# Two encoder layers on one core: layer 0's keys pass DRAM once as float32 and are split on chip

## The chip, the core and the metric

The kernel runs on one core of a Trainium2 chip. Time is the device time of one execution in microseconds (us). The engines have names in the profile: PE is TensorE (matmuls; PEld its weight loads), DVE is VectorE, ACT is ScalarE, POOL is GpSimd, SP is SyncE, whose queue issues nearly all transfers, in order. Tiles lie in SBUF as 128 partitions (rows) by some columns.

## The reference

Two layers of a streaming encoder, for 1024 prompt positions and for 8 streams of 16 new positions with cached keys and values. All is float32.

```python
# layer 0: two attentions side by side, 8 heads of 64 each
qa, ka, va, qb, kb, vb, fa = split(rmsnorm(x) @ w_in_even)
# a: causal, with a forget gate; c = cumsum(log_sigmoid(fa + b_forget))
s = qa @ ka.T / 8 + (c_q - c_k);  s = where(kpos <= qpos, s, -inf)
# b: a band of 8 chunks of 64 to the left, with a bias by clipped distance
s = qb @ kb.T / 8 + bias;         s = where(in_band, s, -inf)
o = softmax(s) @ v;  x += concat(oa, ob) @ w_out;  x += swiglu(rmsnorm(x))
# layer 1: 16 query heads in 2 groups, one key and value head a group, window 128
s = q @ k.T / 8 + t5_bias;  softmax with a learned sink;  x += ... (as above)
y = rmsnorm(x)        # the new keys, values and gates are returned too
```

## The kernel before

Float32 accuracy comes from products in a faster 32-bit format (F32R): an operand is split into a high part (a cast) and a low part (the difference), and three products are summed. `passes` issues them (L191 to L193) for projections and feed-forward. The order of instructions on each engine is fixed when the kernel is built: the program lists steps with costs, `merge` interleaves lists by them, and a scheduler then places the instructions.

Layer 0 starts with the projections. `proj_k` (L369) handles one pair of heads of keys, 128 rows by 1024 positions: it copies the result out, stores it as an output, splits it, and stores the high and the low part to DRAM (`kh`, `kl`). `attn_load` (L456) later loads one head: q (64 rows high, 64 rows low); the keys' high part twice, one below the other; the low part; for kind a also q's high part again (`bt`) and four gate rows each for `bt` and `kl` from `cpd`; for kind b the bias instead. Most tiles have two buffers. Values of two heads share a tile (`vp`) and are split by GpSimd (L484, L485).

`score_step` (L490) takes 128 query rows against up to 512 keys with two products into one sum: L505, q high and low against the doubled high keys (128 rows), and L507, q high against the low keys. For kind a that second product has 68 rows (64 and the gate rows); for kind b it has 64. Then come the softmax (L442 on VectorE, L445 on ScalarE), transposes (L544), a split of the weights (L548, L549), and the products with the values (L574, L575); GpSimd applies the reciprocal sums (L593), which pass DRAM (`rds`). `sample_steps` (L656) is merged between: cached keys and values of one stream (`skt`, `svt`, 1 MB each), bias of kind a (`sbi`, L679), scores (L695), and the values product L720, whose last block has the 16 new positions (`svn`) and 16 rows.

Layer 1's attention is `c_steps` (L834). Keys and values of a group of 8 query heads are loaded when it starts; these tiles have one buffer. Its list has 194 entries, about three to each of 64 units (one pair of query heads by 128 positions). The first `cut` entries, 24/32 of them (L1591), are merged with six of the eight q projections, the rest runs behind. Here the score products are L777 and L778, the transposes L794, and the values products L809 and L810.

Of the kernel before, what the change touches and what calls it, by code (L numbers as in the profile page):

```python
# [11 lines left out]
F32 = mybir.dt.float32  # L12
# [7 lines left out]
P = 128  # L20
# [9 lines left out]
HD = 64  # L30
# [8 lines left out]
VB = 1  # L39
APART = 1  # L40
# [20 lines left out]
def model(ctx: ExitStack, tc: tile.TileContext, I, O):  # L61
# [62 lines left out]
    kh = {k: dr.tile([512, NP], F32, name=f"kh_{k}") for k in "ab"}  # L124
    kl = {k: dr.tile([512, NP], F32, name=f"kl_{k}") for k in "ab"}
    kh["c"] = dr.tile([P, NP], F32, name="kh_c")
    kl["c"] = dr.tile([P, NP], F32, name="kl_c")
# [20 lines left out]
    def nm(s):  # L148
        uid[0] += 1
        return f"{s}_{uid[0]}"  # L150
# [218 lines left out]
    def proj_k(src, act, pool, out, dst_hi, dst_lo, dst_sample, get=ps_any):  # L369
        def finish(o, c0, c1):  # L370
            w = min(c1, NP) - c0
            kf = pool.tile([P, c1 - c0], F32, name=nm("kf"), tag="kf", bufs=2)
            A.copy(kf, o[:, :c1 - c0])
            S.dma_start(out[:, c0:c1], kf)
            kh_ = pool.tile([P, c1 - c0], F32R, name=nm("khs"), tag="sth", bufs=2)
            kl_ = pool.tile([P, c1 - c0], F32R, name=nm("kls"), tag="stl", bufs=2)
            A.copy(kh_[:, :w], o[:, :w])
            V.tensor_tensor(kl_[:, :w], o[:, :w], kh_[:, :w], ALU.subtract)
            S.dma_start(dst_hi[:, c0:c0 + w], f32(kh_)[:, :w])
            S.dma_start(dst_lo[:, c0:c0 + w], f32(kl_)[:, :w])  # L380
            if c1 > NP:
                S.dma_start(dst_sample, kf[:, w:w + NS])

        return chunk_steps(src, act, get, finish, 1)
# [71 lines left out]
    def attn_load(pool, kind, h):  # L456


        tl = lambda z: pool.tile([P, NP], F32R, name=nm(z), tag=z, bufs=2)
        q, kh_, kl_, v = (tl(z) for z in ("q", "kh", "kl", "v"))  # L460
        v = v.rearrange("p (a b) -> p a b", b=P)
        if h % 2 == 0:
            marks["vp"] = pool.tile([P, 8, P], F32, name=nm("vp"), tag="vp", bufs=VB)
        vp = marks["vp"]
        n = 4 if kind == "a" else 0
        rows = slice(h * HD, (h + 1) * HD)
# [4 lines left out]
        bt = pool.tile([P, NP], F32R if n else F32, name=nm("bt"), tag="bt", bufs=2)  # L471
        if n:
            S.dma_start(f32(bt)[n:n + HD], qs[kind][h][:HD])
            S.dma_start(f32(bt)[:n], cpd[h, 0])
            S.dma_start(f32(kl_)[:n], cpd[h, 1])
            q2, kl2, bias = bt[:n + HD], kl_[:n + HD], None
        else:
            S.dma_start(bt[:, :640], I["bias_b"][h])
            G.tensor_scalar(bt[:, :640], bt[:, :640], -1.0, 1.0, ALU.mult, ALU.mult)
# [3 lines left out]
        vp = vp[:, :, h % 2 * HD:(h % 2 + 1) * HD]  # L483
# [172 lines left out]
    def sample_steps(pool, qbd, nbs):  # L656
        st = {}

        def head(kind, hd):
            for z, src in (("q", qsm), ("k", ksm)):  # L660
                hd[z] = pool.tile([P, 4, NS], F32, name=nm(z + "all"), tag=z + "all")
                S.dma_start(hd[z], src[kind])
# [22 lines left out]
        def load_v(kind, b, un):  # L685
            un["vn"] = vn = pool.tile([16, 512], F32, name=nm("svn"), tag="svn", bufs=2)
            S.dma_start(un["vt"], I[f"cache_{kind}_v"][b])
            S.dma_start(vn, vsm[kind][b * 16:(b + 1) * 16, :])
# [13 lines left out]
        def trans(un):  # L702
            un["p"] = pts = pool.tile([P, 5, P], F32, name=nm("spt"), tag="spt", bufs=1)
# [8 lines left out]
        def values(un):  # L712

            op, pts = un["o"], un["p"]
            for kb in range(5):
                for p in range(4):
                    c = slice(p * 32, (p + 1) * 32)
                    lhs = pts[:, kb, c] if kb < 4 else pts[:16, 4, c]
                    rhs = un["vt"][:, kb, p * P:(p + 1) * P] if kb < 4 else un["vn"][:, p * P:(p + 1) * P]
                    E.matmul(op[c, :P], lhs, rhs, start=kb == 0, stop=kb == 4, skip_group_check=True)  # L720
# [113 lines left out]
    def c_steps(pool, qt):  # L834
# [3 lines left out]
        def load(j):  # L838
            kv = j // 4
            if j % 4 == 0:  # L840
                kh_ = pool.tile([P, NP], F32R, name=nm("kh"), tag="kh", bufs=1)
                kl_ = pool.tile([P, NP], F32R, name=nm("kl"), tag="kl", bufs=1)
                v = pool.tile([P, 8, P], F32R, name=nm("v"), tag="v", bufs=1)
# [629 lines left out]
    def unit(ki, p, pool, w=None):  # L1473

        kind = "ab"[ki]
        if p < 4:
# [4 lines left out]
                      kh[kind][p * P:(p + 1) * P], kl[kind][p * P:(p + 1) * P], ksm[kind][:, p, :])  # L1481
# [289 lines left out]
```

## Time and profile before

| | |
|---|---|
| Median of 3 runs | 2781.97 us (2778.57 to 2789.56) |
| Profiled execution, own time | 2780.07 us |
| its span in the profile | 2778.3 us |
| TensorE busy, weight loads busy | 2639.6 us (95%), 2525.9 us (91%) |
| VectorE, GpSimd, ScalarE busy | 60%, 44%, 41% |
| Mean granted TensorE clock | 0.969 of full |
| DMA | 357.65 MB, 129 GB/s over the span |

How to read it: a matmul's end is modelled, so successive starts say more of its cost than its length, and a gap may hide inside "busy". The granted clock is the share of 2.4 GHz that TensorE was given. In a view by stage a row has from:to in us, the length, then busy us and (x instructions) of PE, PEld, DVE, ACT and POOL, the clock, the share of 16 DMA engines, and GB/s. A row in order of time has start, length, engine, line, operation, output<-inputs, shape and, in brackets, the idle time before it and what ended that. A row of waits has total us, times and the longest. A row of groups has count, then busy us, mean ns and idle before.

### The profile page before, as it was taken

What the parts mean: (1) busy time and instruction counts of PE and PEld (TensorE: products, weight loads), DVE (VectorE), ACT (ScalarE), POOL (GpSimd) and SP (SyncE); (2) the same over time, 40 slices, a digit from 0 to 9 for tenths busy, and PEclk for the clock granted to TensorE, in tenths of its full rate; (3) what the DMA queues carried; (4) which work ended last, traced back from release to release, by engine and by line L of the source; (5) the groups of instructions that cost most, each with busy time, mean ns of one, the idle gap of its engine ahead of it and who ended that gap; (6) DMA issues with size and microseconds to landing.
All of it is one profiled execution on the core that took longest, in us unless ns stands there. A gap on an engine that the chain in (4) does not pass through costs nothing.

```text
span 2778.3 us, 52629 instructions
## 1 busy us (share of the span) xinstructions
PE 2639.6 (95%) x19774; PEld 2525.9 (91%) x19774; DVE 1661.7 (60%) x3583; ACT 1139.7 (41%) x2510; POOL 1229.6 (44%) x1120
## 2 busy tenths in 40 slices
PE   8999998998989999999999998869799999999997
PEld 7999976777989999999999998869799999999997
DVE  7110275766685565655667767854956555566666
ACT  5221376776342222223333466754432222233333
POOL 4212122232543343434997532233444344448984
PEclk9999998999989999999999999989999999999998
DMA  5546587885222332326443132332123222355432
GB/s 161 171 136 205 175 232 235 261 278 173 66 74 86 96 104 81 102 83 233 148 119 104 60 113 86 103 104 74 71 71 102 85 98 96 94 179 200 119 96 77
DMA packets 209840, 357.65 MB, mean 129 GB/s; under 512 B 27816, under 2 KB 134448, under 8 KB 207536
## 3 DMA queue, kind: packets, MB, share of 16 engines
q1 hardware_dynamic: 204976, 349.55, 40.6%
q10 hardware_dynamic: 4608, 4.72, 0.5%
q8 instruction: 156, 2.56, 0.4%
q14 instruction: 100, 0.82, 0.1%
HBM read 252.22 MB, written 101.95 MB: 127 GB/s over the span
## 4 chain that ended last, share of the span: by engine, by line
PE 77%; DVE 9%; DMA 7%; issue 2%; ACT 2%; POOL 1%; SPq 1%; DVEq 0%; ACTq 0%; POOLq 0%
PE ps L191 21%; PE ps L192 21%; PE ps L193 20%; PE ps L544 2%; PE ps L507 2%; DVE hf L281 1%; PE ps L505 1%; PE ps L397 1%; PE ps L396 1%; PE ps L398 1%; DMA oraw<-od 1%; PE ps L574 1%; DVE pg L285 1%; PE ps L575 1%; DVE h L281 1%
## 5 line engine op out<-in xcount | busy, mean ns | idle before, releaser
L191 PE MATMUL ps<-pg,wh 128*128 128x288 f32 x3200 | 955.9, 300 | 22.5 <-ACT wh L284 9.9
L192 PE MATMUL ps<-pg,wh 128*128 128x288 f32 x3200 | 951.9, 298 | 3.0 <-POOL pg L285 2.0
L193 PE MATMUL ps<-pg,wh 128*128 128x288 f32 x3200 | 937.1, 296 | 1.4 <-DVE wh L285 1.3
L191 PEld LDWEIGHTS ps<-pg,wh 128*128 128x128 f32 x3200 | 606.3, 190 | 28.3 <-ACT wh L284 11.6
L192 PEld LDWEIGHTS ps<-pg,wh 128*128 128x128 f32 x3200 | 608.2, 190 | 5.4 <-POOL pg L285 2.8
L193 PEld LDWEIGHTS ps<-pg,wh 128*128 128x128 f32 x3200 | 604.0, 190 | 2.7 <-DVE wh L285 2.1
L285 POOL TENSOR_TENSOR wh<-wr,wh 128x1024 fp32r<-128x1024 f32 (+1 forms) x96 | 232.8, 2429 | 327.7 <-ACT wh L284 327.4
L284 ACT CAST wh<-wr 128x1024 fp32r<-128x1024 f32 (+2 forms) x156 | 160.9, 1036 | 249.7 <-PE ps L193 219.7
L191 PE MATMUL ps<-hh,wh 128*128 128x288 f32 x832 | 246.1, 301 | 4.2 <-ACT hh L284 3.1
L192 PE MATMUL ps<-hl,wh 128*128 128x288 f32 x832 | 247.4, 299 | 2.5 <-DVE hl L285 2.3
L193 PE MATMUL ps<-hh,wh 128*128 128x288 f32 x832 | 244.9, 296 | 0.0
L285 POOL TENSOR_TENSOR pg<-pg,pg 128x576 fp32r<-128x576 f32 x126 | 197.1, 1579 | 47.4 <-ACT pg L284 47.1
L1335 DVE TENSOR_TENSOR x<-x,ps 128x288 f32<-128x288 f32 x384 | 158.1, 447 | 89.3 <-PE ps L193 74.8
L284 ACT CAST pg<-pg 128x576 fp32r<-128x576 f32 (+1 forms) x134 | 90.4, 702 | 246.1 <-PE ps L193 106.4
L285 POOL TENSOR_TENSOR wh<-x,wh 128x1024 fp32r<-128x1024 f32 x42 | 100.9, 2403 | 151.4 <-ACT wh L284 151.4
L191 PEld LDWEIGHTS ps<-hh,wh 128*128 128x128 f32 x832 | 156.5, 190 | 8.4 <-ACT hh L284 5.0
L192 PEld LDWEIGHTS ps<-hl,wh 128*128 128x128 f32 x832 | 158.0, 190 | 4.6 <-DVE hl L285 3.6
L193 PEld LDWEIGHTS ps<-hh,wh 128*128 128x128 f32 x832 | 157.9, 190 | 0.1
L285 POOL TENSOR_TENSOR x<-wr,x 128x512 fp32r<-128x512 f32 x44 | 58.7, 1334 | 210.7 <-ACT x L284 210.7
L1191 DVE TENSOR_TENSOR u<-p,ps 128x288 f32<-128x288 f32 x176 | 78.9, 448 | 112.6 <-PE ps L193 112.4
L549 DVE TENSOR_TENSOR pl<-ps,ph 128x512 fp32r<-128x512 f32 (+1 forms) x152 | 92.3, 611 | 33.8 <-ACT ph L548 33.1
L191 PE MATMUL ps<-x,wh 128*128 128x288 f32 x352 | 105.5, 300 | 5.5 <-DVE x L1195 5.3
(298 smaller groups left out, 6166.1 us busy)
## 6 DMA issues: line engine op xcount, KB each, us to landing
wr<-w_ffn_in SPq DMA_DIRECT2D x88, 512.0 KB
hds<-hd SPq DMA_DIRECT2D x252, 144.0 KB
pg<-hds SPq DMA_DIRECT2D x126, 288.0 KB
wd<-w_ffn_out SPq DMA_DIRECT2D x36, 512.0 KB
wr<-w_out SPq DMA_DIRECT2D x22, 512.0 KB
xd<-x SPq DMA_DIRECT2D x16, 576.0 KB
x<-xd SPq DMA_DIRECT2D x16, 576.0 KB
svt<-cache_a_v SPq DMA_DIRECT2D x8, 1024.0 KB
```

Source lines behind the costliest of these rows:

```text
L191: E.matmul(out, wh_, xh_, start=first and i == 0, stop=False, skip_group_check=seen)
L192: E.matmul(out, wh_, xl_, start=False, stop=False, skip_group_check=seen)
L193: E.matmul(out, wl_, xh_, start=False, stop=last and i == n - 1, skip_group_check=seen)
L281: V.scalar_tensor_tensor(out, src, gains[:, gi, k:k + 1], rs, ALU.mult, ALU.mult)
L284: A.copy(hi, src)
L285: eng.tensor_tensor(lo, src, hi, ALU.subtract)
L396: E.matmul(o[:, :width], xh_[:, k], wts[k][0], start=k == 0, stop=False)
L507: E.matmul(sp[:, :w], q2[:, qt], kl2[:, k0:k0 + w], start=False, stop=not dg)
L544: E.transpose(pt[:, col:col + P], tl[:, (kb - kb0) * P:(kb - kb0 + 1) * P], ident)
L549: V.tensor_tensor(fl, pt[:, lo_:hi_], fh, ALU.subtract)
L1191: V.tensor_tensor(st[n, q], st["p1", q], st["x", q][:, :QW], ALU.add)
L1335: V.tensor_tensor(z, z, o, ALU.add)
```

## The change

Layer 0's keys are stored once, as float32 (`ks`), from the tile that also goes to the output. A pair of heads is loaded as one tile (`kp`, two buffers), and GpSimd makes the doubled high part and the low part of each head from it. For kind a the copy of q comes from q's tile, and the gate rows move to rows 64 to 67. For kind b rows 64 to 127 of the low part are set to zero, and the second product runs over all 128 rows. The sample tiles for the 16 new positions get 128 rows, zeroed once at the start. In layer 1 the tiles of keys and values get a second buffer, and `cut` becomes 27/32. The scratch for dynamic DMA is set to 1024.

```diff
@@ proj_k
             S.dma_start(out[:, c0:c1], kf)
+            if c1 > NP:
+                S.dma_start(dst_sample, kf[:, w:w + NS])
+            if dst_lo is None:
+                S.dma_start(dst_hi[:, c0:c0 + w], kf[:, :w])
+                return
             kh_ = pool.tile([P, c1 - c0], F32R, name=nm("khs"), tag="sth", bufs=2)
...
@@ attn_load
         if h % 2 == 0:
+            marks["kp"] = kp = pool.tile([P, NP], F32, name=nm("kp"), tag="kp", bufs=KB)
+            S.dma_start(kp, ks[kind][h * HD:(h + 2) * HD])
             marks["vp"] = pool.tile([P, 8, P], F32, name=nm("vp"), tag="vp", bufs=VB)
...
-        for r in range(2):
-            S.dma_start(f32(kh_)[r * HD:(r + 1) * HD], kh[kind][rows])
-        S.dma_start(f32(kl_)[n:n + HD], kl[kind][rows])
...
-            S.dma_start(f32(bt)[n:n + HD], qs[kind][h][:HD])
-            S.dma_start(f32(bt)[:n], cpd[h, 0])
-            S.dma_start(f32(kl_)[:n], cpd[h, 1])
-            q2, kl2, bias = bt[:n + HD], kl_[:n + HD], None
...
+            S.dma_start(f32(bt)[HD:HD + 4], cpd[h, 0])
+            S.dma_start(f32(kl_)[HD:HD + 4], cpd[h, 1])
...
-            q2, kl2, bias = q[:HD], kl_[:HD], bt
...
+        for r in range(2):
+            G.tensor_copy(kh_[r * HD:(r + 1) * HD], kp[half])
+        G.tensor_tensor(kl_[:HD], kp[half], kh_[half], ALU.subtract)
+        if kind == "a":
+            G.tensor_copy(bt[:HD], q[:HD])
+            q2, kl2, bias = bt[:HD + 4], kl_[:HD + 4], None
+        else:
+            G.memset(f32(kl_)[HD:], 0.0)
+            G.tensor_scalar(bt[:, :640], bt[:, :640], -1.0, 1.0, ALU.mult, ALU.mult)
+            q2, kl2, bias = q, kl_, bt
...
@@ sample_steps
+        vnew = [pool.tile([P, 512], F32, name=f"svn{i}") for i in range(2)]
+        pts = pool.tile([P, 5, P], F32, name="spt")
+        for z in vnew + [pts[:, 4]]:
+            G.memset(z, 0.0)
...
-                    lhs = pts[:, kb, c] if kb < 4 else pts[:16, 4, c]
...
@@ c_steps
-                kh_ = pool.tile([P, NP], F32R, name=nm("kh"), tag="kh", bufs=1)
+                kh_ = pool.tile([P, NP], F32R, name=nm("kh"), tag="kh", bufs=2)
...
@@ model
-        cut = len(cst) * 24 // 32
+        cut = len(cst) * 27 // 32
```

The scheduler gives every engine a new order in these stages. Three places follow; numbers behind a name tell buffers of one tile apart.

The first place is SyncE's queue in kind a, where the fifth head is loaded. Before:

```order
L482 DMA vp_4931<-vs_a 128x8x128
L467 DMA q_4927<-qs_a 128x1024
L594 DMA od_123<-ob_4681 64x512
L469 DMA kh_4928<-kh_a 64x1024 x2
L470 DMA kl_4929<-kl_a 64x1024
L473 DMA bt_4936<-qs_a 64x1024
L474 DMA bt_4936<-cpd 4x1024
L475 DMA kl_4929<-cpd 4x1024
L669 DMA skt_5065<-cache_a_kt 128x4x512
```

And with the change:

```order
L471 DMA q_4770<-qs_a 128x1024
L535 DMA rdb_4561<-rds_a 64x512
L474 DMA bt_4778<-cpd 4x1024
L475 DMA kl_4772<-cpd 4x1024
L681 DMA skt_4908<-cache_a_kt 128x4x512
L121 DMA rds_a<-rt_4511 4x32 x4
L699 DMA svt_4909<-cache_a_v 128x2048
L467 DMA kp_5452<-ks_a 128x1024
```

The head's keys are no longer in this piece: its pair was loaded earlier, and the `kp` here is that of the seventh and eighth head. The two gate loads have no other load of their tiles ahead of them.

The second place is SyncE's queue in layer 1's attention, around the second group's keys (`kh`, `kl`) and values (`v`). Before, they stand among the loads and stores of later units:

```order
L172 DMA wr_22744<-w_out 128x1024
L830 DMA od_124<-ou_20714 128x512
L845 DMA kh_21133<-kh_c 64x1024
L846 DMA kl_21134<-kl_c 64x1024
L845 DMA kh_21133<-kh_c 64x1024
L846 DMA kl_21134<-kl_c 64x1024
L850 DMA bt_21555<-bias_c 128x2x256
```

With the change, right behind the first group's:

```order
L857 DMA v_19392<-vs_c 128x8x128
L860 DMA bt_19398<-bias_c 128x2x256
L860 DMA bt_19717<-bias_c 128x2x256
L855 DMA kh_20918<-kh_c 64x1024
L856 DMA kl_20919<-kl_c 64x1024
L855 DMA kh_20918<-kh_c 64x1024
L856 DMA kl_20919<-kl_c 64x1024
L364 DMA qsm_c<-qf_19387 128x128
L857 DMA v_20920<-vs_c 128x8x128
L171 DMA wr_21692<-w_qc 128x1024
```

They moved ahead of the weights of a q projection (`w_qc`) and of all of the first group's stores.

The third place is GpSimd's queue in kind a. Before, a head's work there is only its values:

```order
L670 COPY skt_5065<-kall_4207 128x4x16
L672 COPY qbd_3931<-qall_4205 64x4x16 x2
L593 TENSOR_TENSOR ob_4819<-ou_4685,rdb_4717 64x2x128 x2
L679 TENSOR_TENSOR sbi_5071<-sbi_5071,cqs 128x528
L484 CAST v_4930<-vp_4931 128x8x64
L680 TENSOR_TENSOR sbi_5071<-sbi_5071,mask_79 128x16
L485 TENSOR_TENSOR v_4930<-vp_4931,v_4930 128x8x64
```

With the change:

```order
L484 COPY bt_4443<-q_4438 64x1024
L691 TENSOR_TENSOR sbi_4316<-sbi_4316,cqs 128x528
L691 TENSOR_TENSOR sbi_4615<-sbi_4615,cqs 128x528
L482 TENSOR_TENSOR kl_4440<-kp_4092,kh_4439 64x1024
L491 CAST v_4441<-vp_4094 128x8x64
L600 TENSOR_TENSOR ob_4525<-ou_4337,rdb_4350 64x2x128 x2
L481 CAST kh_4771<-kp_4774 64x1024 x2
L682 COPY skt_4908<-kall_4053 128x4x16
```

The fourth head's low keys (`kl_4440`) stand behind two steps on the sample bias (`sbi`), and the fifth head's high keys (`kh_4771`) behind a step that needs reciprocals from DRAM (`rdb`).

## Rows read from the trace of the kernel before

**Rows 1.** The page, part 1: busy us, share of span, instructions of each engine.
```profile
PE 2639.6 (95%) x19774; PEld 2525.9 (91%) x19774; DVE 1661.7 (60%) x3583; ACT 1139.7 (41%) x2510; POOL 1229.6 (44%) x1120
```

**Rows 2.** Busy time by stage, columns as told with the profile above.
```profile
200.00:340.00 140.00, 140.00 (x1109) 139.01 (x1108) 16.16 (x47) 34.39 (x84) 23.75 (x16) 1.00 0.61 185
340.00:500.00 160.00, 144.17 (x1216) 112.14 (x1216) 108.40 (x339) 109.33 (x265) 45.86 (x85) 0.91 0.82 236
500.00:660.00 160.00, 159.92 (x1296) 114.40 (x1295) 112.75 (x383) 117.21 (x302) 48.38 (x77) 1.00 0.79 240
660.00:710.00 50.00, 38.59 (x258) 36.69 (x257) 23.59 (x33) 26.34 (x45) 23.37 (x19) 0.86 0.63 193
...
1710.00:1730.00 20.00, 14.32 (x97) 13.54 (x96) 10.12 (x37) 9.63 (x30) 3.69 (x13) 0.83 0.48 128
...
1790.00:1860.00 70.00, 43.20 (x244) 38.02 (x244) 45.10 (x136) 41.02 (x113) 18.05 (x48) 0.76 0.42 127
...
380.00:390.00 10.00, 10.00 (x86) 8.02 (x85) 9.28 (x33) 9.30 (x23) 1.07 (x1) 1.00 0.89 286
```

**Rows 3.** TensorE's waits, 340 to 660 us: total us, times, longest.
```profile
PE ps L507 <- DMA kl<-cpd: 8.7, 3, 4.3
```

**Rows 4.** The chain of waits, 420 to 432 us: start, us, what.
```profile
421.42 8.05 DMA kl<-kl_a
...
429.48 1.85 DMA kl<-cpd
```

**Rows 5.** TensorE's matmuls in order of time, in kind a and kind b.
```profile
348.14 0.34 PE L505 MATMUL ps<-kh,q 128*128 128x384 f32 x1
348.31 0.34 PE L507 MATMUL ps<-kl,bt 68*128 68x384 f32 x1
348.49 0.60 PE L544 MATMUL ps<-ident,t 128*128 128x128 f32 x4
...
571.00 0.34 PE L505 MATMUL ps<-kh,q 128*128 128x384 f32 x1
...
571.63 0.38 PE L505 MATMUL ps<-kh,q 128*128 128x256 f32 x1
...
576.11 0.42 PE L505 MATMUL ps<-kh,q 128*128 128x384 f32 x1
576.46 0.44 PE L507 MATMUL ps<-kl,q 64*128 64x384 f32 x1
576.83 0.55 PE L544 MATMUL ps<-ident,t 128*128 128x128 f32 x3
```

**Rows 6.** Weight loads: the group of L507, 500 to 660 us; one of svn.
```profile
L507 PEld LDWEIGHTS ps<-kl,q 64*128 64x128 f32 x96 | 17.5, 183 | 15.3 <-issue 9.5
...
570.42 0.15 PEld L720 LDWEIGHTS ps<-svn,spt 16*32 16x32 f32 x8 [0.20 <-issue]
```

**Rows 7.** GpSimd's groups by shape, 200 to 660 us.
```profile
L285 POOL TENSOR_TENSOR wh<-wr,wh 128x1024 fp32r<-128x1024 f32 x9 | 21.6, 2409 | 71.5 <-ACT wh L284 71.5
L485 POOL TENSOR_TENSOR v<-vp,v 128x512 fp32r<-128x512 f32 x16 | 20.5, 1282 | 0.4
L484 POOL CAST v<-vp 128x512 fp32r<-128x512 f32 x16 | 9.7, 612 | 23.2 <-DMA vp<-vs_a 17.5 <-DMA vp<-vs_b 2.3 <-PE ps L507 1.8
...
L670 POOL COPY skt<-kall 128x64 f32<-128x64 f32 x16 | 3.7, 235 | 1.4 <-PE ps L695 1.4
```

**Rows 8.** Layer 1 on TensorE: two matmuls, and busy time in projections (hh) alone.
```profile
1724.03 1.01 PE L777 MATMUL ps<-kh,q 128*128 128x128 f32 x3 [5.65 <-DMA kh<-kh_c]
...
1824.72 0.28 PE L810 MATMUL ps<-pl,v 128*128 128x256 f32 x1
...
1625.00:1790.00 165.00, 82.68 (x387) 0.98 0.26 82
```

**Rows 9.** GpSimd's waits, 340 to 660 us: total us, times, longest.
```profile
POOL sbi L679 <- DMA sbi<-csd: 45.1, 6, 13.2
POOL ob L593 <- DMA rdb<-rds_a: 43.0, 8, 11.2
```

More of the change, by code (lines that the diff above doesn't have):

```diff
@@ L39 @@
 VB = 1
+KB = 2
 APART = 1
@@ L123, in model @@
     qs = {k: dr.tile([8, P, NP], F32, name=f"qs_{k}") for k in "ab"}
[L124 to L127, printed above, removed]
+    ks = {k: dr.tile([512, NP], F32, name=f"ks_{k}") for k in "ab"}
+    kh, kl = ({"c": dr.tile([P, NP], F32, name=f"{z}_c")} for z in ("kh", "kl"))
     vs = {k: dr.tile([P, 8, 4, P], F32, name=f"vs_{k}") for k in "ab"}
@@ L462, in attn_load @@
         if h % 2 == 0:
+            marks["kp"] = kp = pool.tile([P, NP], F32, name=nm("kp"), tag="kp", bufs=KB)
+            S.dma_start(kp, ks[kind][h * HD:(h + 2) * HD])
             marks["vp"] = pool.tile([P, 8, P], F32, name=nm("vp"), tag="vp", bufs=VB)
[L464 to L466 removed]
+        kp, vp = marks["kp"], marks["vp"]
+        half = slice(h % 2 * HD, (h % 2 + 1) * HD)
         S.dma_start(f32(q), qs[kind][h])
[L468 to L476 removed]
+        bt = pool.tile([P, NP], F32R if kind == "a" else F32, name=nm("bt"), tag="bt", bufs=2)
+        if kind == "a":
+            S.dma_start(f32(bt)[HD:HD + 4], cpd[h, 0])
+            S.dma_start(f32(kl_)[HD:HD + 4], cpd[h, 1])
         else:
             S.dma_start(bt[:, :640], I["bias_b"][h])
[L479 to L480 removed]
         if h % 2 == 0:
             marks["q"] = S.dma_start(vp, vs[kind][:, :, h // 2, :])
[L483 removed]
+        for r in range(2):
+            G.tensor_copy(kh_[r * HD:(r + 1) * HD], kp[half])
+        G.tensor_tensor(kl_[:HD], kp[half], kh_[half], ALU.subtract)
+        if kind == "a":
+            G.tensor_copy(bt[:HD], q[:HD])
[4 more added lines that the diff above has]
+            q2, kl2, bias = q, kl_, bt
+        vp = vp[:, :, half]
         G.tensor_copy(v[:, :, :HD], vp)
@@ L685, in load_v @@
         def load_v(kind, b, un):
-            un["vn"] = vn = pool.tile([16, 512], F32, name=nm("svn"), tag="svn", bufs=2)
+            un["vn"] = vn = vnew[b % 2]
             S.dma_start(un["vt"], I[f"cache_{kind}_v"][b])
-            S.dma_start(vn, vsm[kind][b * 16:(b + 1) * 16, :])
+            S.dma_start(vn[:16], vsm[kind][b * 16:(b + 1) * 16, :])
         def scores(kind, b, c, un):
@@ L712, in values @@
         def values(un):
-            op, pts = un["o"], un["p"]
+            op = un["o"]
             for kb in range(5):
@@ L717, in values @@
                     c = slice(p * 32, (p + 1) * 32)
-                    lhs = pts[:, kb, c] if kb < 4 else pts[:16, 4, c]
                     rhs = un["vt"][:, kb, p * P:(p + 1) * P] if kb < 4 else un["vn"][:, p * P:(p + 1) * P]
-                    E.matmul(op[c, :P], lhs, rhs, start=kb == 0, stop=kb == 4, skip_group_check=True)
+                    E.matmul(op[c, :P], pts[:, kb, c], rhs, start=kb == 0, stop=kb == 4, skip_group_check=True)
             un["of"] = of = pool.tile([P, P], F32, name=nm("sof"), tag="sof", bufs=1)
@@ L1480, in unit @@
         return proj_k(I["w_k"][ki * 4 + p], act, pool, O[f"{kind}_kt"][p * P:(p + 1) * P],
-                      kh[kind][p * P:(p + 1) * P], kl[kind][p * P:(p + 1) * P], ksm[kind][:, p, :])
+                      ks[kind][p * P:(p + 1) * P], None, ksm[kind][:, p, :])
     flat = lambda ls: [s_ for l in ls for s_ in l]
```

9 lines of the change are left out of this document (3 added, 6 removed).

## The prediction

> **What bounds the kernel now.** I read four views in this order: the page, busy time by stage, TensorE's waits, and single instructions in time order. The page gives TensorE 95% of the span and no other engine more than 60% [rows 1]. So only TensorE's lost time counts: waits, slow clock, and gaps inside what the profile still calls busy. By stage [rows 2] the feed-forward part that fills most of the span is not touched, and three stages are. In the first half of layer 0's attention (340 to 500 us, the heads of kind a, whose matmuls have 68 rows) TensorE is busy 144.2 of 160 us at a mean granted clock of 0.91. In the second half (500 to 660, kind b) it is busy 159.9 of 160 at 1.00, so nothing but TensorE seems to bind there. In layer 1's attention it is 14.3 of 20 at 0.83 in one piece (1710 to 1730), and 43.2 of 70 at 0.76 where that attention ends (1790 to 1860).
>
> In the first of these, TensorE's largest waits have one cause: three waits, 8.7 us, for the four gate rows that are loaded into the tile of the keys' low parts [rows 3]. The chain of waits shows why. The 256 KB load of the low parts takes 8.05 us, the load of gate rows into the same tile starts only when it has landed (1.85 us more), then the matmul runs [rows 4]. SyncE issues in order, so whatever stands behind that load waits too.
>
> **64-row matmuls.** In kind b each score product is a 128-row matmul (L505) and then a 64-row one (L507). For a pair of 384 columns the starts are 576.11, 576.46 and, of the matmul after, 576.83: 0.72 us; from 571.00 to 571.63 it is 0.63. The same pair in kind a, with 68 rows, goes 348.14, 348.31, 348.49: 0.35 us [rows 5]. All three stretches run at full granted clock. So the 64 rows cost 0.28 to 0.37 us a pair, mean 0.32, inside time that counts as busy; the weight loads of L507 show part of it as idle of "issue" (9.5 us over the stage) [rows 6]. There are 96 of them in kind b, all in this stage: 96 x 0.32 = 31 us. The change makes them 128 rows, with zeros below. The sample products with 16 rows (svn) show the same gap of 0.20 us going in [rows 6]; 16 units x 0.20 = 3 us. Together 34 us of TensorE.
>
> Two statements of the Trainium skill bear on this and disagree. "TensorE: Matmul & The Clock Gate", section "Why this matters for your kernels", has it that a matmul with few rows takes as long as one with 128; by that, this part is worth 0 and the sum below would be 20 us instead of 45. "TensorEngine Tiling (Array Packing)", section "Tiling Modes", says that a change of tiling mode drains the engine; by that, the 34 us go. The rows side with the second.
>
> Will the other engines follow? ScalarE is busy 117.2 of those 160 us and VectorE 112.8 [rows 2]; in 126 us ScalarE would be at 93%. The row of 380 to 390 has both at 93% with TensorE at 10.0 of 10 [rows 2], so it can be done for a while, but over eight heads some waits must come up. I take 25, with 34 and 13 as ends: at 13 the stage would take 147 us, with ScalarE at 80%.
>
> **Keys once, split on chip.** Removed loads: for a head of kind a 2 x 256 KB high parts, 256 KB low parts and 256 KB of q (64 rows of 1024 floats each) become half of a 512 KB tile that serves two heads, 768 KB less; for kind b 512 KB less. 8 x 1280 KB = 10.2 MB, at the 236 to 240 GB/s of these stages [rows 2] some 43 us of transfers that ran beside the work. The gate rows now go into tiles that no other load writes, and the SyncE queue has no load before them to wait for (first place shown from the order). So the three waits of 8.7 us should go. The granted clock of this half costs up to 144.2 x 0.09 = 13 us on top of 15.8 us idle, 28 in all. I take the 8.7, a third of the clock's 13, and give 3 back for the new work on GpSimd: 10 us. Ends: 28 if every stall goes, and -10 if GpSimd's queue makes up for all of it.
>
> The new work on GpSimd for a head is two casts, a subtraction and a copy (kind b: a zero fill) of 1024 elements each. The rows of 512 elements are 612 ns for the cast and 1282 for the subtraction, of 64 elements 235 ns for a copy, of 1024 elements 2409 ns for a subtraction [rows 7]. So a cast or copy of 1024 is near 0.61 + 512 x (0.612 - 0.235)/448 = 1.04 us, a head 3 x 1.04 + 2.41 = 5.5 us, sixteen heads 88. A zero fill of this size has no row; it reads nothing, so I bound it by 0 and the copy's 1.04, and take 1.04. GpSimd is busy 45.9 and 48.4 of 160 us in the two halves [rows 2]; with 44 more in each it is at 56 to 73%. That it is in time is the assumption that carries most risk (below).
>
> In the projections 32 casts on ScalarE, 32 subtractions on VectorE and 32 stores go. TensorE is busy 140.0 of 140 us there [rows 2], so this gains 0; if heads 0 and 1 keep GpSimd from the weights' low parts, that costs at most the few 2.4 us splits of the weights. GpSimd's fills of the sample tiles happen once, and the smaller scratch for DMA changes no queue that the page shows. Both 0.
>
> **Layer 1.** TensorE waits 5.65 us for the second group's keys; their loads wait until the first group's only tile is free; the granted clock of the 20 us around it is 0.83 [rows 2, 8]. With two buffers these loads stand right behind the first group's (second place shown). The wait goes, and so do 14.3 x 0.17 = 2.4 us of slow clock: 8 us. The spread moves 3/32 of 194 entries, six of 64 units, from behind the q projections to beside them. The projections take 82.7 us of TensorE between 1625 and 1790 [rows 8], so a unit costs (165 - 5.7 - 82.7)/48 = 1.6 us there. Behind them 16 units last from 1790 to 1824.7 [rows 8], 2.2 us each. Six moved units give 6 x 0.6 = 3.6 us; as the last loads of the output projection's weights are still there, I take 2. Layer 1: 10, ends 5 and 14.
>
> **The sum.** 25 + 10 + 10 = 45. The profiled execution took 2780.1 us, 0.07% below the median of the runs, so I compare with either: 2780 - 45 = 2735.
>
> **Rivals.**
> - *GpSimd's queue decides; slower.* Now a head's keys wait behind everything on GpSimd. That engine waits for loads: 45.1 us in six waits for the sample bias, longest 13.2, and 43.0 in eight for the softmax reciprocals, longest 11.2 [rows 9]. Nobody waited for GpSimd then. Now the keys' subtraction stands right behind two bias steps (third place shown). For it: these waits are as long as half a head. Against: tiles have two buffers, so a head's work may start about 20 us before it is needed, and the loads are fewer. Each us that a head comes late costs 14 us over fourteen heads; from 45/14 = 3.2 us on the change loses. At 5 us: 2735 + 70 = 2805.
> - *ScalarE and the transfers take over.* Half of the 34 us goes to waits for ScalarE, the first half gains nothing: 13 + 0 + 9 = 22, 2758. For it: ScalarE's 93%, and DMA busy 0.79 to 0.82 as a mean [rows 2].
> - *The 64 rows are not the cause.* The gap is due to something else, such as the weight loads, and stays with 128 rows. This is what the Trainium skill's first statement above would make of it. 10 + 10 = 20, so 2760. Against: the 68-row pair has the same order of loads and no gap.
> - *Everything is cleared.* 34 + 28 + 12 = 74: 2706.
> - That the change doesn't do what it says I put at nothing: the order shows the keys' loads gone and the early second group.
>
> **How the numbers follow.** Forecast 0.60, cleared 0.11, ScalarE 0.17, 64 rows 0.05, GpSimd 0.07. A measurement of this kernel tells 0.5%, 14 us, from no change: the line is at 2768. Forecast and cleared lie below it, and most of the two middle cases; with their spread 0.85 faster, 0.09 within, 0.06 slower. The range leaves out GpSimd's case and the far end of the cleared one, and takes the ends of the terms: 2710 to 2770.
>
> **What would show it.** Right: in kind b pairs of 384 columns start 0.35 us apart in sum, with the stage near 135 us instead of 160; no wait for gate rows; no wait for the second group's keys; GpSimd at 55 to 75% in layer 0's attention. Wrong: TensorE waits for GpSimd's key tiles for 3 us a head or more, the gaps stay, or the time saved comes back as idle before the output projection, where TensorE is busy 38.6 of 50 us now [rows 2].

## The result and the profile after

| | before | changed | ratio, 95% interval |
|---|---|---|---|
| time, median (range), us | 2780.74 (2778.57 to 2789.56) | 2732.05 (2730.97 to 2735.86) | 0.9826 [0.9809, 0.9842] |
| span of the profiled execution, us | 2778.3 | 2729.2 | |
| mean granted clock of TensorE | 0.969 | 0.977 | |

The kernel became faster by 48.7 us, 1.75%. The forecast was 2735 us in a range of 2710 to 2770, so the time lies 3 us from it.

The page of the changed kernel, its span and part 1 (busy us, share of the span, instructions), stands against [rows 1]:

```profile
span 2729.2 us, 52425 instructions
PE 2597.0 (95%) x19774; PEld 2511.3 (92%) x19774; DVE 1651.6 (61%) x3551; ACT 1128.9 (41%) x2478; POOL 1314.2 (48%) x1187
```

TensorE has as many instructions as before and is busy 42.6 us (2639.6 - 2597.0) less. VectorE and ScalarE have lost 32 instructions each, the splits of the keys in the projections. GpSimd has gained 67 instructions and 85 us of work (the prediction's estimate was 88). TensorE's share stays at 95%, and no other engine passes 61%, so it is still the bound. By the two pages the transfers fell from 357.65 to 342.93 MB; what is read from DRAM fell by 10.5 MB (the prediction worked out 10.2).

To see where the time went, I read from each trace when an instruction that marks a stage starts. On TensorE these are the first or last matmul of a kind. The gate-up stage, the first part of a feed-forward, is taken from VectorE's first sum of two weight tiles. Layer 0's end is taken from VectorE's first sum of squares behind it, and the last row from its last one. The columns are one profiled execution each, in us:

| | before | changed | shift |
|---|---|---|---|
| layer 0's projections end | 336.5 | 336.8 | +0.3 |
| last score product of kind a | 501.2 | 484.6 | -16.6 |
| last value product of layer 0's attention | 664.4 | 627.9 | -36.5 |
| first matmul of the output projection | 673.1 | 634.7 | -38.4 |
| first sum of the gate-up stage | 741.5 | 699.3 | -42.2 |
| layer 0 ends | 1538.7 | 1491.0 | -47.7 |
| first sum of layer 1's gate-up stage | 1930.9 | 1879.3 | -51.6 |
| last normalisation | 2760.1 | 2710.6 | -49.5 |

Three quarters of the gain, 36.5 us, stand at the end of layer 0's attention: 16.6 in kind a and 19.9 in kind b. Another 11.2 come between there and layer 0's end, in a part of the code that the change does not touch. Layer 1's stretch up to its gate-up stage brings 3.9, and 2.1 are lost again behind it.

Busy time by stage of the changed kernel, with the columns of [rows 2] (stretch, length, busy us of PE, PEld, DVE, ACT, POOL, granted clock, DMA share, GB/s), for kind a, kind b and the start of the gate-up stage:

```profile
340.00:485.00 145.00, 137.77 (x1223) 108.48 (x1221) 110.20 (x343) 109.94 (x266) 86.41 (x117) 0.96 0.73 236
485.00:619.00 134.00, 128.40 (x1234) 106.64 (x1232) 106.80 (x368) 111.74 (x290) 81.63 (x100) 1.00 0.71 236
...
698.00:759.00 61.00, 56.40 (x416) 55.50 (x415) 55.98 (x100) 26.09 (x58) 28.65 (x27) 1.00 0.22 89
```

In kind a TensorE's idle time fell from 15.8 to 7.2 us and its granted clock rose from 0.91 to 0.96. In kind b TensorE is busy 128.4 of 134 us at a clock of 1.00, where the row before had 159.9 of 160 at the same clock. (That row also holds a few us of the work on either side, 1296 matmul records against 1234, so the size is taken from the table above. From its first score product to its last, kind b takes 151.8 us before, 502.4 to 654.2, and 133.8 now, 485.0 to 618.8.) Time that counted as busy has gone. GpSimd is at 60 and 61% of the two halves, and ScalarE at 83% of the second. The last row is a piece outside of attention. In the kernel before, the same work stands in this row,

```profile
740.00:805.00 65.00, 60.39 (x413) 59.24 (x412) 55.71 (x100) 25.61 (x56) 28.66 (x27) 0.92 0.22 85
```

at a granted clock of 0.92 instead of 1.00 and 4 us longer. Why the clock differs is not shown: in the variants below that piece has 1.00 in some and 0.97 in others, also where only layer 1 was changed (0.97 in e6_cut24, 1.00 in e5_one_buffer).

TensorE in time order in kind b (start, length, engine, line, what), against the last three lines of [rows 5]:

```profile
562.31 0.34 PE L512 MATMUL ps<-kh,q 128*128 128x384 f32 x1
562.49 0.34 PE L514 MATMUL ps<-kl,q 128*128 128x384 f32 x1
562.67 0.49 PE L551 MATMUL ps<-ident,t 128*128 128x128 f32 x3
```

From 562.31 to 562.67 the pair takes 0.36 us, where it took 0.72. The weight loads of the second product, against the first line of [rows 6] (busy us, mean ns, idle before and its cause), show the same:

```profile
L514 PEld LDWEIGHTS ps<-kl,q 128*128 128x128 f32 x96 | 17.7, 189 | 0.0
```

The 9.5 us of idle time "issue" are now 0.0.

TensorE's waits from 330 to 700 us (total us, times, longest), against [rows 3]:

```profile
PE ps L190 <- ACT wh L283: 6.6, 1, 6.6
PE ps L512 <- DVE smins L444: 2.8, 4, 1.9
PE ps L512 <- DVE mins L444: 2.5, 5, 0.8
PE ps L551 <- ACT t L447: 2.0, 6, 0.5
PE ps L551 <- DVE pl L556: 1.8, 7, 0.5
```

The wait for the gate rows (8.7 us in three) is gone, and none for GpSimd's key tiles has come. What is left inside attention is many small waits, most of them for the softmax on VectorE and ScalarE. The 6.6 us are at the start of the output projection.

GpSimd's groups in the attention of layer 0 (busy us, mean ns, idle before) give the prices that the prediction had worked out from [rows 7]:

```profile
L482 POOL TENSOR_TENSOR kl<-kp,kh 64x1024 fp32r<-64x1024 f32 x14 | 33.3, 2379 | 0.6
L481 POOL CAST kh<-kp 64x1024 fp32r<-64x1024 f32 x28 | 29.0, 1036 | 7.4 <-PE ps L514 3.7 <-PE ps L512 2.8
L487 POOL MEMSET kl<- 64x1024 f32 x8 | 7.6, 949 | 0.0
L484 POOL CAST bt<-q 64x1024 fp32r<-64x1024 f32 x6 | 6.2, 1036 | 10.8 <-DMA q<-qs_a 6.4 <-PE ps L582 4.3
```

The cast was put at 1.04 us and takes 1.036, the subtraction at 2.41 and takes 2.379, the zero fill, which had no row, at up to 1.04 and takes 0.949. A head has two casts, a subtraction and a copy or fill: 5.4 to 5.5 us.

In layer 1, TensorE's waits from 1560 to 1920 us:

```profile
PE ps L926 <- POOL bs_c L899: 11.8, 1, 11.8
PE ps L787 <- DVE mins L768: 7.4, 8, 2.4
PE ps L804 <- DVE pl L809: 5.7, 5, 2.7
```

The wait for the second group's keys [rows 8] is gone, but a single wait of 11.8 us now leads. The timeline around it (start, length, engine or queue, what; in brackets idle before and its cause):

```profile
1795.08 1.26 POOL L839 TENSOR_TENSOR ou<-ou,rdb 128x512 f32<-128x512 f32 x1 [9.85 <-DMA rdb<-rds_c]
1796.37 0.34 SPq L840 DMA_DIRECT2D od<-ou  x1
1798.15 0.62 SPq L889 DMA_DIRECT2D bs_c<-bias_cs  x1
1799.76 0.43 SPq L916 DMA_DIRECT2D kt_c<-ksm_c  x1
1802.93 1.30 PE L926 MATMUL ps<-kt_c,qb_c 128*128 128x144 f32 x4 [11.82 <-POOL bs_c L899]
```

GpSimd waits 9.85 us for the last heads' reciprocals (`rdb`), which pass DRAM. Then it scales these heads' output, SyncE stores it, and only then the loads for the sample's score product are issued; that product (L926) runs 3.2 us after them. In the kernel before, the sample's score products waited as well, but in two places:

```profile
1836.79 1.30 PE L916 MATMUL ps<-kt_c,qb_c 128*128 128x144 f32 x4 [4.86 <-DMA kt_c<-ksm_c]
1841.37 0.28 PE L810 MATMUL ps<-pl,v 128*128 128x256 f32 x1
1860.55 0.82 PE L916 MATMUL ps<-kt_c,qb_c 128*128 128x144 f32 x2 [5.88 <-DVE x L1006]
```

The middle line is the last value product of layer 1's attention. In the changed kernel it is this one, ahead of the sample's first score product:

```profile
1783.74 0.28 PE L820 MATMUL ps<-pl,v 128*128 128x256 f32 x1
```

So before, 4.9 us were waited inside the attention and 5.9 behind it, 10.7 in all; now it is 11.8, all of it behind the attention.

### The profile page after: what moved, and what is told of

The parts are those of the page before. It is cut to its first block, busy times and chain, and to the rows that moved or that the text cites. A ratio compares the mean times of both kernels' runs of the same rounds, so it can differ in the third digit from the quotient of the medians.

```text
span 2729.2 us, 52425 instructions
## 1 busy us (share of the span) xinstructions
PE 2597.0 (95%) x19774; PEld 2511.3 (92%) x19774; DVE 1651.6 (61%) x3551; ACT 1128.9 (41%) x2478; POOL 1314.2 (48%) x1187
## 2 busy tenths in 40 slices
DMA packets 201901, 342.93 MB, mean 126 GB/s; under 512 B 26536, under 2 KB 129072, under 8 KB 199600
## 5 line engine op out<-in xcount | busy, mean ns | idle before, releaser
L283 ACT CAST wh<-wr 128x1024 fp32r<-128x1024 f32 (+2 forms) x156 | 161.0, 1036 | 246.1 <-PE ps L192 216.8
```

Source lines behind the costliest of these rows:

```text
L283: A.copy(hi, src)
```

## The experiments

The scheduler orders each kernel anew, so differences of a few us between variants are not those of the edit alone. Every ratio is against executions of the kernel before that were taken beside the variant; the changed kernel's is 0.9826 [0.9809, 0.9842]. Differences in us are those of the medians unless said otherwise. The median of the kernel before itself moved between 2779 and 2785 us from one set of runs to the next, so such a difference is uncertain by a few us, and by the ratios it can come out otherwise.

**Second product of kind b on 64 rows again (e1_rows64)**

```diff
-            G.memset(f32(kl_)[HD:], 0.0)
-            q2, kl2, bias = q, kl_, bt
+            q2, kl2, bias = q[:HD], kl_[:HD], bt
```

> The changed kernel with the second score product of kind b on 64 rows again (no zero fill). Theory (a matmul on fewer rows than the one before it leaves a gap going in and coming out): a pair of 384 columns takes 0.63 to 0.72 us again, kind b's scores take some 150 us from first to last instead of 129, and the time is 2750 to 2760 us, 18 to 28 above the changed kernel. Rival (the gap isn't due to the rows; kind b got faster because of its loads): within 5 us of the changed kernel's 2732.

Measured: 2756.14 us, 0.9902 [0.9888, 0.9917]; 24 us slower than the changed kernel (21 by the ratios), as the theory had it. TensorE in time order in kind b:

```profile
560.11 0.34 PE L511 MATMUL ps<-kh,q 128*128 128x384 f32 x1
560.38 0.44 PE L513 MATMUL ps<-kl,q 64*128 64x384 f32 x1
560.75 0.38 PE L511 MATMUL ps<-kh,q 128*128 128x256 f32 x1
```

The weight loads of that product, and the stage:

```profile
L513 PEld LDWEIGHTS ps<-kl,q 64*128 64x128 f32 x96 | 17.1, 183 | 15.3 <-issue 9.9 <-POOL ob L599 0.2 <-POOL qbd L683 0.2
```

```profile
487.00:643.00 156.00, 154.90 (x1233) 112.29 (x1232) 109.21 (x371) 113.55 (x290) 75.87 (x93) 0.99 0.62 204
```

The pair is back at 0.64 us (another in the same trace takes 0.72), and the 9.9 us of "issue" are back. Apart from the scheduler's order nothing but the row count and the fill differs, so the gap belongs to the 64 rows. (The 129 us in the expectation count the second products alone, 490.0 to 618.8 us in the changed kernel; counted so, they take 151.5 us here.) In this stage TensorE is busy 26.5 us more than in the changed kernel (154.9 against 128.4) and idle 4.5 less (1.1 against 5.6): 26.5 - 4.5 = 22 us. That is how a gain of TensorE time turns into a smaller one of stage time: 4.5 us come back as waits, most of them for the softmax.

**Keys stored and loaded in two parts again (e2_loads), and both parts undone (e3_neither)**

```diff
-            marks["kp"] = kp = pool.tile([P, NP], F32, name=nm("kp"), tag="kp", bufs=KB)
-            S.dma_start(kp, ks[kind][h * HD:(h + 2) * HD])
...
+        for r in range(2):
+            S.dma_start(f32(kh_)[r * HD:(r + 1) * HD], kh[kind][rows])
+        S.dma_start(f32(kl_)[:HD], kl[kind][rows])
...
+            S.dma_start(f32(bt)[:HD], qs[kind][h][:HD])
...
-        for r in range(2):
-            G.tensor_copy(kh_[r * HD:(r + 1) * HD], kp[half])
-        G.tensor_tensor(kl_[:HD], kp[half], kh_[half], ALU.subtract)
...
-            G.tensor_copy(bt[:HD], q[:HD])
```

(With it the projections store both parts for kinds a and b again; e3_neither is this and the edit of e1_rows64 together.)

> The changed kernel with layer 0's keys stored and loaded as two parts again, in the changed kernel's rows (gate rows last, 128-row products). Theory (loads and the wait on a load into the same tile hold up kind a): TensorE waits for the gate rows again, kind a ends some 10 to 16 us later, time 2742 to 2752 us. Rival (the 128-row products alone made the gain, in kind a the new order did): within 5 us of 2732.

> Both undone: keys in two parts from DRAM and 64-row products; layer 1 and the sample tiles as changed. If the two parts add up: 2765 to 2778 us, the sum of what each alone gave back, and what is left below the kernel before (2 to 16 us) is the worth of layer 1 and the sample tiles. Rival (they overlap, one hides the other's worth): clearly less than the sum of the two.

Measured: e2_loads 2761.05 us, 0.9925 [0.9907, 0.9943], 29 us slower than the changed kernel, where the theory had 10 to 20. e3_neither 2766.68 us, 0.9949 [0.9931, 0.9967], 35 us slower. The waits of e2_loads from 330 to 700 us:

```profile
PE ps L515 <- DMA kl<-cpd: 6.8, 3, 3.3
...
PE ps L513 <- DMA kh<-kh_b: 4.2, 2, 3.5
PE ps L708 <- DMA skt<-cache_a_kt: 3.4, 1, 3.4
PE ps L515 <- DMA kl<-kl_b: 3.1, 4, 1.1
```

Its two halves:

```profile
340.00:499.00 159.00, 142.53 (x1229) 111.72 (x1229) 109.92 (x342) 110.63 (x268) 46.76 (x86) 0.95 0.83 240
499.00:645.00 146.00, 130.65 (x1220) 110.68 (x1219) 103.91 (x366) 109.95 (x287) 53.60 (x81) 0.94 0.81 247
```

The gate rows' wait of kind a is back, and kind a ends 14.1 us later than in the changed kernel, both as expected. Not expected is kind b: its products have 128 rows here, so TensorE needs only 130.7 us, but the stage takes 146. TensorE waits 7.3 us for the keys' two parts (kh<-kh_b, kl<-kl_b), its granted clock is 0.94, and the DMA engines are at 0.81. In the changed kernel they are at 0.71, the clock at 1.00, and the stage takes 134.

So the two parts do not add. From e3_neither, the 128 rows alone give 2766.68 - 2761.05 = 5.6 us, the single pass of the keys alone gives 2766.68 - 2756.14 = 10.5, and both give 34.6. The 18.5 us between 34.6 and 5.6 + 10.5 need both. By the ratios the four numbers are 7, 13, 34 and 14 us, and the intervals leave the 14 uncertain by some 9. The time of e3_neither lies in the range that was stated for parts that add, but what each gave back alone, 24 and 29 us, makes 53 and not 35, so the rival's case came. The traces say in which stage (us; kind a until its last score product, kind b from there to the last value product of layer 0's attention):

| | kind a ends | kind b takes |
|---|---|---|
| both parts (changed kernel) | 484.6 | 143.3 |
| single pass of the keys alone (e1_rows64) | 487.0 | 165.3 |
| 128 rows alone (e2_loads) | 498.7 | 156.5 |
| neither (e3_neither) | 501.4 | 164.9 |

In kind a the single pass gives 14 us with either row count. In kind b it gives nothing while the products have 64 rows (165.3 against 164.9), the 128 rows alone give 8.4 us, and both give 21.6: the 13 to 14 us that need both stand there. As I read the traces, with the 64-row gap TensorE is the bound of kind b and has no use for fewer loads; without the gap the loads become the bound if they stay as they were.

What is left of the change in e3_neither (layer 1 and the sample tiles) is worth some 14 us against the kernel before, more than the 8 and 2 us that the next runs find for these. Its profile is of the slowest of its five executions, 9 us above the median, and does not show where these 14 us stand.

**GpSimd's work on the keys twice (e7_twice), its subtraction alone twice (e11_subtract_twice)**

```diff
+            for _ in range(2):
                 G.tensor_copy(kh_[r * HD:(r + 1) * HD], kp[half])
+        for _ in range(2):
             G.tensor_tensor(kl_[:HD], kp[half], kh_[half], ALU.subtract)
```

(e11_subtract_twice has the second loop only.)

> The changed kernel with GpSimd's two casts and the subtraction of each head's keys done twice into the same tiles: 2 x 1.04 + 2.4 = 4.5 us more on GpSimd for each head, 72 us in all. Theory (the keys are made well ahead, GpSimd has slack): under 5 us more than 2732, no wait of TensorE for GpSimd over 1 us. Rival (GpSimd's queue is near deciding): TensorE waits for the key tiles, 15 us or more.

> Only the subtraction of each head's keys done twice on GpSimd, 2.4 us more a head (38 us in all), about half of what the run with all three doubled added; that one cost 67 us. Theory (GpSimd only costs when its time for a head passes the head's time on TensorE, some 16 to 18 us; here it is near 13): under 6 us more than 2732, no wait for the key tiles over 2 us. Rival (its waits for loads leave no room, each us a head shows): 25 us or more, with waits for the key tiles.

Measured: e7_twice (2 x 1.04 + 2.38 = 4.5 us more for a head) 2799.2 us, 1.0059 [1.0044, 1.0074], slower than the kernel before and 67 us slower than the changed one. e11_subtract_twice (2.4 us more) 2740.63 us, 0.986 [0.9841, 0.988], 9 us slower than the changed one; its profile is of its fastest execution, 2734.68 us. First e7_twice, the wait that leads and the two halves:

```profile
PE ps L516 <- POOL kl L484: 49.5, 6, 11.5
```

```profile
340.00:522.00 182.00, 150.09 (x1234) 115.96 (x1232) 113.35 (x344) 112.05 (x270) 118.57 (x139) 0.88 0.62 197
522.00:683.00 161.00, 133.78 (x1220) 111.48 (x1221) 107.40 (x367) 110.92 (x289) 112.43 (x120) 0.92 0.57 184
```

Then e11_subtract_twice, the same:

```profile
PE ps L515 <- POOL kl L483: 6.4, 3, 2.9
```

```profile
340.00:487.00 147.00, 139.64 (x1247) 109.14 (x1250) 114.08 (x351) 111.92 (x272) 103.37 (x125) 0.99 0.76 243
487.00:621.00 134.00, 124.34 (x1181) 103.05 (x1174) 102.21 (x348) 106.07 (x277) 97.80 (x105) 0.97 0.66 217
```

At 2.4 us more a head TensorE waits 6.4 us for GpSimd's tile, and layer 0's attention ends 6.4 us later (last value product at 634.3 instead of 627.9). At 4.5 us more TensorE waits 49.5 us for that tile, its clock falls to 0.88 in the first half, attention ends at 692.6, which is 64.7 of the 67 us, and the rival on GpSimd's queue has come true. For e11_subtract_twice neither came: 9 us is more than the theory's 6 and less than the rival's 25, and the longest wait for the tile is 2.9 us. In e7_twice GpSimd is busy only 65 and 70% of the two halves. It takes its work in the order fixed in the kernel, and in between it waits too: in these halves 22.4 us for the sample's bias from DRAM, and 17.7 and 16.7 us for TensorE to be done with the tiles of earlier keys and values. So it held TensorE up long before its busy share said so. The first 2.4 us a head (38 us in all) cost 8.6 us of time, the next 2.1 (33 in all) cost 58.6: what the changed kernel has to spare is less than 2.4 us for a head of some 17, and beyond that the price climbs steeply.

**Sample products on 16 rows again (e4_sample16)**

```diff
-                    rhs = un["vt"][:, kb, p * P:(p + 1) * P] if kb < 4 else un["vn"][:, p * P:(p + 1) * P]
-                    E.matmul(op[c, :P], pts[:, kb, c], rhs, start=kb == 0, stop=kb == 4, skip_group_check=True)
+                    rhs = un["vt"][:, kb, p * P:(p + 1) * P] if kb < 4 else un["vn"][:16, p * P:(p + 1) * P]
+                    lhs = pts[:, kb, c] if kb < 4 else pts[:16, 4, c]
+                    E.matmul(op[c, :P], lhs, rhs, start=kb == 0, stop=kb == 4, skip_group_check=True)
```

> The changed kernel with the last block of the sample values product on 16 rows again. Theory (one more gap of 0.2 us a unit): 16 x 0.2 = 3 us more than 2732. Rival (hidden beside other waits): within 1 us.

Measured: 2734.76 us, 0.9822 [0.9809, 0.9836]. By time the two kernels can't be told apart: 2.7 us slower by the medians, 1 us faster by the ratios. The traces do tell them apart. The weight loads of the sample's new values (idle before them until: us, times), in e4_sample16:

```profile
  issue: 2.7, 13
```

In the changed kernel the same group has 0.4 us, once. The 2.3 us between them are the gap that the prediction put at 3; whether they reach the kernel's time is not shown.

**Layer 1: one buffer (e5_one_buffer), the old spread (e6_cut24), both (e9_layer1_before)**

```diff
-                kh_ = pool.tile([P, NP], F32R, name=nm("kh"), tag="kh", bufs=2)
+                kh_ = pool.tile([P, NP], F32R, name=nm("kh"), tag="kh", bufs=1)
```

```diff
-        cut = len(cst) * 27 // 32
+        cut = len(cst) * 24 // 32
```

(The first is e5_one_buffer, with kl and v alike; the second e6_cut24; both together e9_layer1_before.)

> The changed kernel with one buffer for layer 1's keys and values. Theory (the wait for the second group's keys costs what it lasts, and the clock after it): that wait of 5 to 6 us is back and the time is 2737 to 2740 us. Rival (layer 1's end is set by SyncE's queue and the sample's loads behind it, so the wait saved is given back there): within 3 us of 2732.

> The changed kernel with 24/32 of layer 1's list beside the q projections again. Theory (six units are cheaper beside the projections): 2 to 4 us more than 2732. Rival (the spread only moves the point at which the last store blocks SyncE's queue): within 2 us, or faster.

> The changed kernel with layer 1 as it was: one buffer for keys and values, and 24/32 of the list beside the projections. Alone, one buffer cost 11 us and 24/32 cost 3 (both by the medians, against the changed kernel's 2732). Theory from the two profiles (the stretch from layer 0's end to layer 1's feed-forward part was 392.2 us before and 388.3 after): layer 1's part is worth 4 us, so 2734 to 2738 us. Rival (it is worth what the forecast said): 2742 us or more.

Measured: e5_one_buffer 2743.27 us, 0.9853 [0.9839, 0.9866]; e6_cut24 2735.4 us, 0.9824 [0.981, 0.9837]; e9_layer1_before 2739.41 us, 0.9856 [0.984, 0.9872]. By the ratios (difference times 2781 us) the second buffer is worth 7.5 us, the spread nothing, and both together 8.3; the intervals of e5_one_buffer and e9_layer1_before just touch that of the changed kernel, so this is a size with an uncertainty of several us. (By the medians the spread costs the 3 us that its theory had; by the ratio it costs nothing.) The traces give a smaller size. From layer 0's end to layer 1's gate-up stage the two kernels with the old layer 1 take 392.2 (before) and 394.1 us (e9_layer1_before). The seven in which layer 1 is that of the changed kernel, itself and e1, e2, e3, e4, e7 and e11, take 385.7 to 391.7, mean 388.8. TensorE's waits of e9_layer1_before from 1560 to 1930 us:

```profile
PE ps L819 <- ACT ph L808: 10.8, 5, 5.0
PE ps L926 <- DMA kt_c<-ksm_c: 4.8, 1, 4.8
```

Where the old layer 1 comes back, so do the waits for ScalarE's part of the softmax (10.8 us, against 1.5 in the changed kernel) and the short 4.8 us wait of the first sample product, against 11.8. The wait for the second group's keys does not come back as expected: all waits for that group's loads are 0.9 us in e5_one_buffer and 2.3 us in e9_layer1_before, where the kernel before had 5.65. In e5_one_buffer the waits for the softmax and its sums are longer instead (5.4 us in L819 for `ou`, against 0.5). So the second buffer is worth some us, but not by that wait alone; why the rest is lost without it is not shown.

**The 11.8 us wait: other queue (e8_act_queue), later sample (e10_sample_later)**

```diff
-            S.dma_start(t, src)
+            A.dma_start(t, src)
...
-            S.dma_start(kt[:, :P], I["cache_c_kt"][b])
...
+            Q = S if b else A
+            Q.dma_start(kt[:, :P], I["cache_c_kt"][b])
...
```

```diff
-            run(merge(steps[0], load(1) + load(2), other[:len(other) // 2]))
+            run(merge(steps[0], load(1) + load(2), [(7000, lambda: None)] + other[:len(other) // 2]))
```

(The first is e8_act_queue: ScalarE issues the sample's bias and query loads and those of its first keys and values. The second is e10_sample_later: an empty step ahead of the sample's other steps.)

> The changed kernel with the first loads of layer 1's sample part issued by ScalarE instead of SyncE. In the changed kernel SyncE waits about 8 us to issue the last store of attention outputs, those loads stand behind it, and TensorE waits 11.8 us for the bias made from one of them. Theory (the order in SyncE's queue costs this time): that wait falls to 4 us or less and the time to 2722 to 2727 us. Rival (the output projection waits for that last store anyway): the wait moves to the output projection's first matmuls, time within 2 us of 2732.

> The changed kernel with layer 1's sample steps entered later: an empty step of cost 7000 ahead of them, so that 96 instead of 29 matmuls of the output projection stand before the first sample product in TensorE's order. Theory (TensorE, in order, waits 11.8 us for the sample's loads while work of the output projection lies ready behind): that wait falls below 3 us, time 2721 to 2726 us. Rival (the output projection's own inputs are late too): the wait goes to its matmuls, within 2 us of 2732.

Measured: e8_act_queue 2733.93 us, 0.9818 [0.9804, 0.9833], the same as the changed kernel. e10_sample_later 2740.62 us, 0.9863 [0.9845, 0.9881], 9 us slower, where its theory had 6 to 11 us less. The timeline of e8_act_queue:

```profile
1795.38 0.73 ACTq L889 DMA_DIRECT2D bs_c<-bias_cs  x1
...
1801.88 1.26 POOL L839 TENSOR_TENSOR ou<-ou,rdb 128x512 f32<-128x512 f32 x1 [12.14 <-DMA rdb<-rds_c]
1803.17 0.35 SPq L840 DMA_DIRECT2D od<-ou  x1
...
1804.69 0.43 POOL L899 TENSOR_SCALAR bs_c<-bs_c 128x288 f32<-128x288 f32 x1
...
1805.19 0.33 ACTq L916 DMA_DIRECT2D kt_c<-cache_c_kt  x1
...
1808.82 1.30 PE L927 MATMUL ps<-kt_c,qb_c 128*128 128x144 f32 x4 [11.29 <-DMA kt_c<-ksm_c]
```

The loads now stand in ScalarE's queue. The bias (bs_c) is loaded early, but GpSimd's step on it (L899) stands behind the step that waits 12.14 us for the reciprocals. The keys' load (kt_c) is still issued only 2 us after the store of the heads' output, and the wait is 11.3 us for it. So SyncE's order alone is not what holds the sample, and that theory falls. The rival had the time right, within 2 us, but the wait stayed with the sample and did not move to the output projection. In e10_sample_later the waits of the first sample product are

```profile
PE ps L926 <- DMA kt_c<-ksm_c: 7.5, 1, 7.5
...
PE ps L926 <- DVE x L1016: 4.0, 1, 4.0
```

which is 11.5 us together: the wait was divided, not shortened, and both theories missed. Common to the three traces is GpSimd's wait for the last reciprocals' way through DRAM: 9.85 us in the changed kernel, 12.14 in e8_act_queue, 10.59 in e10_sample_later. Each time the sample's bias and keys come only behind it, through SyncE's queue or GpSimd's. No run shortens that way, so that it is the cause is argued, not shown. What holds the keys' load in ScalarE's queue is open; that their tile takes memory which something ahead of the store still holds would fit, and was not tried. No variant beats the changed kernel.

## Why the prediction was right

**Kind b, 25 us: right in size and cause, but not on its own.** The stage was forecast "near 135" us and takes 134, the pair 0.35 us and takes 0.36, and the shift is 19.9 us by the table, 22 against e1_rows64. The whole 31 us did not come out. The 96 gaps were put at 0.32 us each; the stage of e1_rows64 has 26.5 us more of busy TensorE, 0.28 a pair. Of these, 4.5 come back as waits, for the reason given: the softmax. ScalarE went to 83%, not 93%. Two statements of the Trainium skill had been set against each other, and e1_rows64 decides for these shapes: with the 64-row product between 128-row ones the kernel is 24 us slower. So the Trainium skill's statement in "TensorE: Matmul & The Clock Gate", section "Why this matters for your kernels" (a single matmul with few rows takes as long as one with 128), by which this part was worth nothing, does not carry over to a sequence that mixes the two. The Trainium skill's statement in "TensorEngine Tiling (Array Packing)", section "Tiling Modes" (a change of mode drains the engine), fits the gap of 0.28 to 0.37 us a pair; that a drain is what makes the gap, no run here shows.

**What the prediction had wrong is the plain sum of kind b and keys.** It added 25 for the rows and 10 for the keys, as if each stood alone. Alone they give 5.6 and 10.5; together 34.6. It had named transfers as a limit only in the rival on ScalarE and the transfers, and e2_loads is that rival with the loads kept: kind b at 146 us. The sum was near (35 forecast, 36.5 by the table) because the change makes both at once.

**Kind a, 10 us: 16.6.** The 8.7 us of waits went as said: TensorE's idle time fell by 8.6. Of the slow clock a third was taken, 4.3 us. TensorE's busy time fell by 6.4, and at 0.91 and 0.96 the work is the same (144.2 x 0.91 = 131, 137.8 x 0.96 = 132), so the clock gave 6.4. The 3 us held back for GpSimd were not needed. 8.6 + 6.4 = 15.0, the stretch from 340 us on. That this comes from the loads is shown by e2_loads, where kind a ends 14.1 us later.

**Layer 1, 10 us: 4 to 8.** The wait for the second group's keys went. Counted from layer 0's end, the last value product of layer 1's attention starts 10.0 us earlier, 292.7 us after it instead of 302.7. Behind it 6.1 are lost again: the output projection with the sample in it takes 95.6 us up to the gate-up stage instead of 89.5, and 11.8 us of wait stand there where 5.9 stood. The prediction had no term for that part. The table gives 3.9, the runs 8. The terms of the 10 are less sure than their sum: the buffer's wait does not come back in e5_one_buffer, and the spread's 2 us can't be told from nothing (e6_cut24). One reading behind the spread was wrong: the units behind the projections do not end at 1824.7 us. The last value product starts at 1841.37, so a unit there takes 3.2 us and not 2.2, with the 4.9 us wait for the sample inside.

**Not foreseen: 11.2 us between attention and layer 0's end**, 1.9 before the output projection, 3.8 in it and 5.5 from the gate-up stage on, where the granted clock of the first 61 us is 1.00 instead of 0.92. The piece in the output projection (68.4 us before, 64.6 in the changed kernel) goes with the single pass of the keys: 64.4 in e1_rows64, 67.2 in e2_loads, 67.7 in e3_neither; but it is 70.1 in e7_twice, which has the single pass too. The last piece (797.2 and 791.7 us) can't be put down to either part: it is 792.8 in e1_rows64, 789.7 in e2_loads and 796.7 in e3_neither, but it moves from 791.4 (e5_one_buffer) to 795.1 (e8_act_queue) also where layer 1 alone is varied. Why the 11.2 us are gained is not settled; that the scheduler orders the work there differently is only a guess, and it was not tried by itself.

**The nearness is partly luck.** Against 25, 10, 10 and nothing for the rest, the table has 19.9, 16.6, 3.9 and 9.1 (11.2 less the 2.1 lost behind layer 1). Kind b and layer 1 fell short by 11, and kind a and the part that nobody forecast made up for it. By mechanism the prediction was right in kinds a and b.

**The rivals.** GpSimd's queue: a real mechanism, not reached; it was said to lose from 3.2 us of lateness a head on, and the runs put the point at which the kernel is no faster than before between 2.4 and 4.5 us of added work a head. Its sign, waits for the key tiles of 3 us a head, appears in e7_twice (49.5 us over 16 heads); in e11_subtract_twice it is 0.4 a head, in the changed kernel nothing. The 64 rows as no cause: fell with e1_rows64. Everything cleared (2706): no, since the softmax's waits and layer 1's end remain. Of the signs for being right, all came: no gate-row wait, none for the second group's keys, GpSimd at 60 and 61% where 55 to 75 was said, and kind b's pairs 0.36 us apart; nor did the time saved come back before the output projection, which starts 38.4 us earlier.

## What to carry to other kernels

Read the start times of neighbouring matmuls before believing a stage that is 100% busy: here 0.3 us a pair was hidden inside busy time, and the other rows for comparison stood in the same trace. Gains on an engine and on its loads need not add: undo each alone and both together, as the two parts here gave 5.6, 10.5 and 34.6 us, and read in the traces in which stage they need each other. And when work is given to an engine whose other steps wait for loads and for free tiles, test its margin by doubling that work. Its busy share says little: GpSimd was at 60% here, at 70 and 73% where more work cost 9 us, and at 65 and 70% where it cost 67.

## What the runs showed of the hardware that was not expected

On GpSimd, a subtraction of 64x1024 with rounding to fp32r takes 2379 ns, 2.3 times the cast of one tile of that size (1036), and a zero fill, which reads nothing, still 949.
